# Squares for two RMS norms taken by ScalarE activations in place of GpSimd multiplications

## The chip, the cores and the metric

The kernel runs on one core of a Trainium2 chip. The core has five instruction queues that work side by side and wait for one another by semaphores: TensorE (PE, matrix products), VectorE (DVE, elementwise work), ScalarE (ACT, activations and copies), GpSimd (POOL, elementwise work here) and SyncE (SP, which issues the transfers, DMAs). Each queue runs its instructions strictly in the order in which the program lists them. The metric is the device time of one execution in microseconds (us); less is better.

## What is computed

One layer of a hybrid decoder on 1024 tokens with 1024 features, all in float32. An RMS norm and one input projection feed two groups of heads: a chunked state-space part (SSD) whose output is gated by SiLU of `z`, and an attention without softmax ("stick-breaking": sigmoids and a running product over the keys). Each group's output gets an RMS norm of its own, which needs the sum of the squares of its 1024 features for every token:

```python
y_ssd = rmsnorm(y * jax.nn.silu(z), ssd_norm_g)
y_att = stick_breaking_attention(q, k, v)
y_att = rmsnorm(y_att.reshape(b, L, D_ATT), att_norm_g)
x = x + jnp.concatenate([y_ssd, y_att], axis=-1) @ w_out
```

Then come a squared-ReLU MLP on a further norm, and a final norm. The change concerns the squares that feed `y_ssd`'s and `y_att`'s norms.

## The kernel before, in words

Activations are kept with the features on the 128 partitions and the tokens along the free axis. Every large product is made from three matrix products of split operands (a rounded part `hi` and the remainder `lo`), as in lines 161 to 163, so PE carries most of the time. Weights come from DRAM in 128x512 blocks `raw` (pool `ws`, two buffers) and are split into `whi` and `wlo`, either by POOL (lines 107 and 108) or by ACT and DVE (lines 110 and 112); a `raw` buffer is free for the next load when its remainder has been made.

**SSD stage (0 to about 380 us).** For each of four groups of heads `ssd_group` (lines 328 to 407) runs interleaved with the projections of the next group. It works through eight chunks; per chunk PE transposes, multiplies the masked decay matrix `wm` (made on DVE and ACT, line 352 is its exponential, line 353 its product with `cbm`) by the inputs, updates the running `state` (DVE, lines 389 and 392) and adds the skip term (line 402). With the last group runs `zgroup` (lines 409 to 426): the projections of the first four 128-feature blocks of `z`, one SiLU over all four (line 418), and then for each block `j` the load of that block's SSD output `yl` from DRAM (line 421, three buffers), the gating product in place in `zb` (DVE, line 422), its store (line 423), the square into `yl` (POOL, line 424) and the addition to the running sum `zacc` (POOL, line 425).

**Attention stage (about 380 to 950 us).** `qkv(hp)` projects q, k and v for a pair of heads; eight pairs follow one another. A `Group` makes the scores (lines 528 to 531), two sigmoids per tile on ACT (lines 548, 549), the running product over the keys on DVE (a scan, line 539) and a product (line 541), transposes of the weights on PE (line 599) with a split of the result on ACT and DVE (`ath`, `atl`, lines 602 and 603), and the products with v (lines 615, 616). `store` (lines 619 to 634) puts the two halves of a PSUM result together: an ACT copy into `y2` (line 628) and a DVE addition into `yt` (line 629) for each head; after the second head of the pair `yt` is stored, squared into `y2` (POOL, line 633) and added to `sacc` (POOL, line 634). There are four such places in a pair. The projections of the next pair run as filler between the attention's pieces, by a hand-made quota with costs per piece; in the eighth pair the filler is `zgate(j)` for the last four blocks of `z` (lines 636 to 650): per half of 512 tokens a load of `yl`, the projection, a sigmoid (ACT, line 644), its product with the projection (DVE, line 645), the gating product (POOL, line 646), the store, the square into `zs` (POOL, line 648) and the addition to `zacc` (POOL, line 649). `yl`, `zs` and `vt` share one set of three buffers (tag `half`), so the next half's sigmoid has to wait until an older half's last reader is done.

**After it.** `mix_operands(0)` loads and splits the first blocks of `w_out` (lines 756, 110 and 112), `mix_block(0)` multiplies them (lines 734 to 736), with the sums of four blocks left in PSUM; `token_scale(zacc)` (lines 715 to 720) turns the sums of squares into scales by way of PE, ACT and POOL, and line 783 adds each scaled PSUM block to `x1`. The norm and the MLP follow.

The framework decides the order of each engine's instructions at compile time: in the order of the text, what stands under `tc.high_priority(offset=HP)` moved 100 places forward, and by when its own model of durations has the inputs ready. The squares stand outside `high_priority`.

Of the kernel before, what the change touches and what calls it, by code (L numbers as in the profile page):

```python
# [11 lines left out]
AF = mybir.ActivationFunctionType  # L12
ALU = mybir.AluOpType
# [37 lines left out]
def trunk(ctx: ExitStack, tc, x, wct, wdt, cols, g_mix, g_mlp, g_fin, wout, wup, wdown, out):  # L51
    nc = tc.nc
    mm, act, vec, pool = nc.tensor.matmul, nc.scalar, nc.vector, nc.gpsimd
# [32 lines left out]
    def wide(name):  # L86
        return pa.tile([P, 1028], F32, name=name, tag="wide", bufs=3)
# [26 lines left out]
    def unit(src, where):  # L114

        parts = []
        for j in range(2):
            raw = ws.tile([P, 512], F32, name="raw", tag="raw", bufs=2)
            nc.sync.dma_start(out=raw, in_=src[:, j * 512:j * 512 + 512])
            hi = ws.tile([P, 512], F32R, name="whi", tag="whi", bufs=NW)  # L120
            lo = ws.tile([P, 512], F32R, name="wlo", tag="wlo", bufs=NW)
            split(raw, hi, lo, where)
            parts.append((hi, lo))
        return parts
# [26 lines left out]
    def gemm_steps(w, hhi, hlo, half, cuts=1):  # L151

        ps = bank("mm")
        m = 512 // cuts
        for q in range(cuts):
            n = slice(half * 512 + q * m, half * 512 + q * m + m)
            o = ps[:, q * m:q * m + m]
            for k in range(KT):
                whi, wlo = w[k // 4]
                wc = slice(k % 4 * P, (k % 4 + 1) * P)  # L160
                mm(out=o, lhsT=whi[:, wc], rhs=hhi[:, k, n], start=(k == 0), stop=False)  # L161
                mm(out=o, lhsT=whi[:, wc], rhs=hlo[:, k, n], start=False, stop=False)  # L162
                mm(out=o, lhsT=wlo[:, wc], rhs=hhi[:, k, n], start=False, stop=(k == KT - 1))  # L163
                if k < KT - 1 or q < cuts - 1:
                    yield
        return ps

    def gemm_half(w, hhi, hlo, half, cuts=1):
        steps = gemm_steps(w, hhi, hlo, half, cuts)
        while True:  # L170
            try:
                next(steps)
            except StopIteration as done:
                return done.value
# [234 lines left out]
    def zgroup():  # L409

        zb = pa.tile([P, 4, T], F32, name="xb", tag="xb", bufs=2)
        for j in range(NZ):
            w = unit(wct[40 + j], "pool")
            for half in range(2):
                ps = gemm_half(w, hhi, hlo, half)
                act.copy(out=zb[:, j, half * 512:half * 512 + 512], in_=ps)
                yield
        act.activation(out=zb[:, 0:NZ], in_=zb[:, 0:NZ], func=AF.Silu)
        for j in range(NZ):
            yl = wide("yl")[:, 0:T]  # L420
            nc.sync.dma_start(out=yl, in_=ysp[j])
            vec.tensor_tensor(out=zb[:, j, :], in0=zb[:, j, :], in1=yl, op=ALU.mult)
            nc.sync.dma_start(out=ygt[j], in_=zb[:, j, :])
            pool.tensor_tensor(out=yl, in0=zb[:, j, :], in1=zb[:, j, :], op=ALU.mult)
            pool.tensor_tensor(out=zacc, in0=zacc, in1=yl, op=ALU.add)
            yield

# [11 lines left out]
    for g in range(4):  # L439
        drive(ssd_group(g, *made[-1]), conv_group(g + 1) if g < 3 else zgroup(), 0.8 if g == 3 else 0.6)  # L440
# [72 lines left out]
    class Group:  # L513
# [106 lines left out]
        def store(self, r, yp):  # L620
            hp, g = self.hp, self.g
            rows = slice(r * 64, r * 64 + 64)
            if r == 0:
                yts[hp, g] = (pb.tile([P, 256], F32, name="yt", tag="yt", bufs=2),
                              pb.tile([P, 256], F32, name="y2", tag="y2", bufs=2))
            yt, y2 = yts[hp, g]
            with tc.high_priority(offset=HP):
                act.copy(out=y2[rows], in_=yp[64:128])
                vec.tensor_tensor(out=yt[rows], in0=yp[0:64], in1=y2[rows], op=ALU.add)
            if r == 1:  # L630
                n = slice(g * 256, g * 256 + 256)
                nc.sync.dma_start(out=ygt[8 + hp, :, n], in_=yt)
                pool.tensor_tensor(out=y2, in0=yt, in1=yt, op=ALU.mult)
                pool.tensor_tensor(out=sacc[:, n], in0=sacc[:, n], in1=y2, op=ALU.add)

    def zgate(j):
        w = unit(wct[40 + j], "pool")
        for half in range(2):
            n = slice(half * 512, half * 512 + 512)
            yl = pb.tile([P, 512], F32, name="yl", tag="half", bufs=NH2)  # L640
            nc.sync.dma_start(out=yl, in_=ysp[j, :, n])
            ps = yield from gemm_steps(w, hhi, hlo, half)
            zs = pb.tile([P, 512], F32, name="zs", tag="half", bufs=NH2)
            act.activation(out=zs, in_=ps, func=AF.Sigmoid)
            vec.tensor_tensor(out=zs, in0=ps, in1=zs, op=ALU.mult)
            pool.tensor_tensor(out=yl, in0=yl, in1=zs, op=ALU.mult)
            nc.sync.dma_start(out=ygt[j, :, n], in_=yl)
            pool.tensor_tensor(out=zs, in0=yl, in1=yl, op=ALU.mult)
            pool.tensor_tensor(out=zacc[:, n], in0=zacc[:, n], in1=zs, op=ALU.add)
            yield  # L650

# [31 lines left out]
    for k in range(len(slots) + LATE):  # L683
        if k < len(slots):
            n, r, b = slots[k]
            hp, at = divmod(k, nslot)
            if at == 0:
                if fill is not None:
                    for _ in fill:
                        run_later()  # L690
                fill = qkv(hp + 1) if hp < 7 else chain(*[zgate(j) for j in range(NZ, 8)])
                nfill = 48 if hp < 7 else (8 - NZ) * 16
                done, used = 0, 0.0
                length = (25.6 + nfill * 0.65) / nslot
            parts = [(0.44, lambda: groups[n].turn(r, b))] + ahead.get(k, [])
        else:
            parts, at = [], nslot - 1
        if k >= LATE:
            n0, r0, b0 = slots[k - LATE]
            parts.append((0.44, lambda: groups[n0].product(r0, b0)))  # L700
        used += sum(c for c, _ in parts)
        quota = min(nfill, max(done, ((at + 1) * length - used) / 0.65))
        had = done
        for i, (_, step) in enumerate(parts):
            step()
            while done + 0.5 < had + (quota - had) * (i + 1) / len(parts):
                next(fill, None)
                run_later()
                done += 1
# [13 lines left out]
    def accumulate(ahl, whl, store, lag=0):  # L723

        late = []
        for tt in range(8):
            for nh in range(2):
                ps = bank("a")
                n = slice(nh * 512, nh * 512 + 512)
                t = slice(tt * P, (tt + 1) * P)  # L730
                nk = len(ahl)
                for k in range(nk):
                    (ah, al), (wh, wl) = ahl[k], whl[k]
                    mm(out=ps, lhsT=ah[:, t], rhs=wh[:, n], start=(k == 0), stop=False)  # L734
                    mm(out=ps, lhsT=ah[:, t], rhs=wl[:, n], start=False, stop=False)  # L735
                    mm(out=ps, lhsT=al[:, t], rhs=wh[:, n], start=False, stop=(k == nk - 1))  # L736
                late.append((ps, tt, n))
                if len(late) == max(1, lag):
                    yield
                    store(*late.pop(0))  # L740
        for args in late:
            store(*args)
# [532 lines left out]
```

## Time and profile before

| | us |
|---|---|
| median of 3 runs (1786.0 to 1787.95) | 1786.34 |
| the profiled execution | 1790.58 |
| its span, first to last instruction | 1788.8 |
| PE busy | 1719.3 |
| DVE busy | 1288.9 |
| ACT busy | 794.7 |
| POOL busy | 572.3 |

The span is what the trace covers; the execution's own time is 1.78 us more. Busy time is the union of an engine's instructions, waiting not counted, but an instruction that is held up after its start counts as busy. An idle time is put down to the instruction whose end came last. The chain of waits goes from the last instruction back to what released it, step by step.

### The profile page before, as it was taken

Reading aid. Unit: us, or ns where it says so; the run is one execution under the profiler, and the core shown is the slowest. Engines: PE = TensorE matmul, PEld = TensorE weight load, DVE = VectorE, ACT = ScalarE, POOL = GpSimd, SP = SyncE. Lnnn points to the kernel's source line nnn. Section 1 sums busy time; section 2 is a strip of 40 time slices with the busy share of each in tenths; the row PEclk is TensorE's granted clock in tenths of the full one; section 3 lists DMA queues with packets and bytes.
Section 4 is the critical chain, followed back from the end, with each engine's and each line's share of the span. In section 5 each row is a group of like instructions: output and inputs, shape, how many; then the busy total and the mean of one; then the engine's idle time right before and its main releaser. Section 6 shows DMA issues by size and latency. Waiting matters only on the chain.

```text
span 1788.8 us, 23877 instructions
## 1 busy us (share of the span) xinstructions
PE 1719.3 (96%) x8492; PEld 1401.2 (78%) x8492; DVE 1288.9 (72%) x1771; ACT 794.7 (44%) x1516; POOL 572.3 (32%) x645
## 2 busy tenths in 40 slices
PE   6999999989999999999989999999999999999997
PEld 5778878767778778778778788778888877888886
DVE  6587886559797888888775665967666656687775
ACT  5232123316566556556542221544455446444443
POOL 6222222154454454554575331410212210010221
PEclk9999999989999999999999999999999999999999
DMA  4101102120011111110135221455433448854554
GB/s 156 36 30 53 56 28 95 59 83 30 30 33 34 35 35 33 33 32 31 58 119 206 95 100 66 151 172 205 160 141 142 151 160 303 292 159 149 165 169 147
DMA packets 90840, 189.40 MB, mean 106 GB/s; under 512 B 10080, under 2 KB 14432, under 8 KB 90720
## 3 DMA queue, kind: packets, MB, share of 16 engines
q1 hardware_dynamic: 90576, 187.61, 30.7%
q8 instruction: 67, 1.10, 0.3%
q14 instruction: 53, 0.43, 0.1%
q10 hardware_dynamic: 144, 0.26, 0.0%
HBM read 137.50 MB, written 50.33 MB: 105 GB/s over the span
## 4 chain that ended last, share of the span: by engine, by line
PE 77%; DVE 13%; POOL 3%; ACT 3%; issue 2%; DMA 2%; SPq 0%; DVEq 0%; POOLq 0%; ACTq 0%
PE ps_mm L163 7%; PE ps_mm L161 7%; PE ps_mm L162 7%; DVE m L539 5%; PE ps_a L1179 4%; PE ps_a L1181 4%; PE ps_a L1180 4%; PE ps_a L734 3%; PE ps_a L736 3%; PE ps_a L735 3%; PE ps_x L987 3%; PE ps_x L986 2%; PE ps_x L985 2%; DVE a L541 2%; PE ps_tr L599 2%
## 5 line engine op out<-in xcount | busy, mean ns | idle before, releaser
L161 PE MATMUL ps_mm<-hhi,whi 128*128 128x512 f32 (+1 forms) x784 | 322.7, 412 | 0.1
L163 PE MATMUL ps_mm<-hhi,wlo 128*128 128x512 f32 (+1 forms) x784 | 309.4, 395 | 0.0
L162 PE MATMUL ps_mm<-hlo,whi 128*128 128x512 f32 (+1 forms) x784 | 308.5, 393 | 0.0
L539 DVE TENSOR_TENSOR_SCAN m<-m 128x512 f32<-128x512 f32 (+7 forms) x128 | 181.1, 1439 | 26.6 <-ACT m L548 26.4
L163 PEld LDWEIGHTS ps_mm<-hhi,wlo 128*128 128x128 f32 x784 | 148.9, 190 | 32.2 <-issue 2.4
L161 PEld LDWEIGHTS ps_mm<-hhi,whi 128*128 128x128 f32 x784 | 149.6, 191 | 20.1 <-issue 2.9
L162 PEld LDWEIGHTS ps_mm<-hlo,whi 128*128 128x128 f32 x784 | 149.6, 191 | 18.5 <-issue 1.4
L112 POOL TENSOR_TENSOR wlo<-wf,whi 128x512 fp32r<-128x512 f32 x48 | 65.8, 1372 | 245.7 <-ACT whi L110 245.7
L107 POOL TENSOR_SCALAR whi<-raw 128x512 fp32r<-128x512 f32 x90 | 66.4, 738 | 218.9 <-PE ps_mm L162 206.2
L108 POOL TENSOR_TENSOR wlo<-raw,whi 128x512 fp32r<-128x512 f32 x90 | 133.6, 1484 | 7.4
L783 DVE SCALAR_TENSOR_TENSOR x<-ps_a,rr,x 128x512 f32<-128x512 f32 x128 | 93.7, 748 | 55.7 <-PE ps_a L736 46.5
L110 ACT CAST op<-raw 128x512 fp32r<-128x512 f32 x131 | 77.9, 620 | 117.0 <-issue 54.8
L603 DVE TENSOR_TENSOR atl<-ps_tr,ath 128x512 fp32r<-128x512 f32 (+1 forms) x160 | 100.6, 630 | 35.2 <-ACT ath L602 33.4
L112 DVE TENSOR_TENSOR op<-raw,op 128x512 fp32r<-128x512 f32 x131 | 93.0, 731 | 41.6 <-ACT op L110 41.2
L548 ACT ACTIVATE m<-ps_a 128x384 f32<-128x384 f32 (+1 forms) x192 | 95.9, 500 | 32.8 <-PE ps_a L531 29.0
L1179 PE MATMUL ps_a<-op 128*128 128x512 f32 x278 | 108.3, 390 | 1.8 <-ACT uP L951 1.8
L599 PE MATMUL ps_tr<-ident,a 128*128 128x128 f32 x576 | 91.6, 275 | 18.6 <-DVE atl L603 10.2
L1181 PE MATMUL ps_a<-op 128*128 128x512 f32 x278 | 108.2, 389 | 0.0
L1180 PE MATMUL ps_a<-op 128*128 128x512 f32 x278 | 108.2, 389 | 0.0
L602 ACT CAST ath<-ps_tr 128x512 fp32r<-128x512 f32 (+1 forms) x160 | 86.8, 544 | 44.0 <-PE ps_tr L599 40.6
L1136 POOL TENSOR_TENSOR x<-x,raw 128x512 f32<-128x512 f32 x16 | 24.5, 1537 | 253.8 <-DVE x L1144 113.7
L599 PEld LDWEIGHTS ps_tr<-ident,a 128*128 128x128 f32 x576 | 70.6, 140 | 41.6 <-DVE atl L603 14.1
(365 smaller groups left out, 4341.7 us busy)
## 6 DMA issues: line engine op xcount, KB each, us to landing
raw<-ub SPq DMA_DIRECT2D x112, 256.0 KB, 3.2
raw<-in_wct_dram SPq DMA_DIRECT2D x96, 256.0 KB, 2.6
wf<-in_wup_dram SPq DMA_DIRECT2D x38, 512.0 KB, 3.5
raw<-in_wdown_dram SPq DMA_DIRECT2D x68, 256.0 KB, 3.4
ub<-v SPq DMA_DIRECT2D x48, 256.0 KB, 2.0
raw<-in_wout_dram SPq DMA_DIRECT2D x32, 256.0 KB, 2.8
yl<-ygt SPq DMA_DIRECT2D x16, 512.0 KB, 3.9
ub<-uP SPq DMA_DIRECT2D x32, 256.0 KB, 2.0
```

Of the source, the lines that this page charges most:

```text
L108: pool.tensor_tensor(out=lo, in0=raw, in1=hi.bitcast(F32), op=ALU.subtract)
L112: e.tensor_tensor(out=lo, in0=raw, in1=hi.bitcast(F32), op=ALU.subtract)
L161: mm(out=o, lhsT=whi[:, wc], rhs=hhi[:, k, n], start=(k == 0), stop=False)
L162: mm(out=o, lhsT=whi[:, wc], rhs=hlo[:, k, n], start=False, stop=False)
L163: mm(out=o, lhsT=wlo[:, wc], rhs=hhi[:, k, n], start=False, stop=(k == KT - 1))
L539: vec.tensor_tensor_scan(mv, mv, mv, 1.0, ALU.mult, ALU.min)
L548: act.activation(out=m[:, o:o + w], in_=src, func=AF.Sigmoid, scale=-1.0)
L599: nc.tensor.transpose(out=tp[:, o:o + P], in_=a[:, c:c + P], identity=ident)
L603: vec.tensor_tensor(out=tl[:, o:], in0=tp[:, o:], in1=th[:, o:].bitcast(F32), op=ALU.subtract)
L1179: mm(out=ps, lhsT=o[0][:, t], rhs=o[2], start=first, stop=False)
L1180: mm(out=ps, lhsT=o[0][:, t], rhs=o[3], start=False, stop=False)
L1181: mm(out=ps, lhsT=o[1][:, t], rhs=o[2], start=False, stop=last)
```

## The change

Three POOL multiplications of a tile with itself become ACT activations with the function Square; sources, destinations and everything around them stay.

```diff
@@ zgroup
             vec.tensor_tensor(out=zb[:, j, :], in0=zb[:, j, :], in1=yl, op=ALU.mult)
             nc.sync.dma_start(out=ygt[j], in_=zb[:, j, :])
-            pool.tensor_tensor(out=yl, in0=zb[:, j, :], in1=zb[:, j, :], op=ALU.mult)
+            act.activation(out=yl, in_=zb[:, j, :], func=AF.Square)
             pool.tensor_tensor(out=zacc, in0=zacc, in1=yl, op=ALU.add)
@@ Group.store
                 nc.sync.dma_start(out=ygt[8 + hp, :, n], in_=yt)
-                pool.tensor_tensor(out=y2, in0=yt, in1=yt, op=ALU.mult)
+                act.activation(out=y2, in_=yt, func=AF.Square)
                 pool.tensor_tensor(out=sacc[:, n], in0=sacc[:, n], in1=y2, op=ALU.add)
@@ zgate
             nc.sync.dma_start(out=ygt[j, :, n], in_=yl)
-            pool.tensor_tensor(out=zs, in0=yl, in1=yl, op=ALU.mult)
+            act.activation(out=zs, in_=yl, func=AF.Square)
             pool.tensor_tensor(out=zacc[:, n], in0=zacc[:, n], in1=zs, op=ALU.add)
```

## Rows read from the trace of the kernel before

**Rows 1.** The page: busy time by engine; the chain that ended last, by engine.

```profile
PE 1719.3 (96%) x8492; PEld 1401.2 (78%) x8492; DVE 1288.9 (72%) x1771; ACT 794.7 (44%) x1516; POOL 572.3 (32%) x645
PE 77%; DVE 13%; POOL 3%; ACT 3%; issue 2%; DMA 2%; SPq 0%; DVEq 0%; POOLq 0%; ACTq 0%
```

**Rows 2.** Stage windows: us; PE, PEld, DVE, ACT, POOL busy (instructions); PEclk, DMA share, GB/s.

```profile
345.00:400.00 55.00, 46.83 (x213) 37.41 (x212) 34.08 (x45) 15.24 (x21) 27.04 (x17) 0.91 0.25 96
646.40:711.80 65.40, 63.42 (x369) 51.98 (x368) 55.52 (x67) 40.55 (x91) 31.84 (x45) 1.00 0.11 33
865.00:953.00 88.00, 83.12 (x447) 68.50 (x445) 58.49 (x67) 39.41 (x86) 63.15 (x60) 0.96 0.32 104
```

**Rows 3.** The same windows in steps of 5 us, the end of the SSD.

```profile
355.00:360.00 5.00, 2.59 (x15) 1.89 (x13) 5.00 (x3) 0.54 (x3) 4.92 (x3) 1.00 0.49 197
375.00:380.00 5.00, 2.05 (x6) 1.76 (x7) 3.73 (x5) 0.58 (x1) 2.44 (x2) 0.52 0.30 105
```

**Rows 4.** POOL's lines 424 and 425: duration ns min/median/max, first and last start.

```profile
L424 POOL TENSOR_TENSOR yl<-xb x4: 1892/2204/2807, 354.1 to 371.9; 128x1024 f32<-128x1024 f32 x4
L425 POOL TENSOR_TENSOR zacc<-zacc,yl x4: 2375/2667/3235, 357.0 to 373.9; 128x1024 f32<-128x1024 f32 x4
```

**Rows 5.** The chain of waits, 355 to 378 us: start, us, what.

```profile
355.15 5.06 DVE wm L353 x2
...
368.06 1.98 DVE state L389
...
372.50 4.60 DVE wlo L112 x2
```

**Rows 6.** DVE's lines 353 and 389 over the whole span: duration ns min/median/max.

```profile
L353 DVE TENSOR_TENSOR wm<-wm,cbm x32: 676/679/2826, 99.9 to 357.4; 128x512 f32<-128x512 f32 x32
L389 DVE TENSOR_TENSOR state<-state,cdn x24: 406/416/2062, 106.1 to 368.0; 128x256 f32<-128x256 f32 x24
```

**Rows 7.** ACT's squares (lines 135, 951) and last table load: ns min/median/max, first and last start.

```profile
L135 ACT ACTIVATE sq<-xq x8: 1056/1060/1078, 4.2 to 23.3; 128x1024 f32<-128x1024 f32 x8
L951 ACT ACTIVATE uP<-uP x16: 631/633/636, 1202.0 to 1456.2; 128x512 f32<-128x512 f32 x16
L548 ACT ACT_TABLE_LOAD  x1: 1283/1283/1283, 404.7 to 404.7; - x1
```

**Rows 8.** POOL 881 to 915 us, by line: busy us, mean ns; and one wait, 860:960.

```profile
L648 POOL TENSOR_TENSOR zs<-yl 128x512 f32<-128x512 f32 x3 | 6.2, 2062 | 0.2
...
ACT zs L644 <- POOL zacc L649: 12.4, 5, 3.8
```

**Rows 9.** 905 to 923 us: the chain's DMA; ACT's timeline; two windows.

```profile
912.59 3.05 DMA raw<-in_wout_dram
...
915.66 0.62 ACT L110 CAST kl<-raw 128x512 fp32r<-128x512 f32 x1 [10.59 <-DMA raw<-in_wout_dram]
...
913.00:918.00 5.00, 1.50 (x9) 0.97 (x7) 1.44 (x3) 2.29 (x5) 1.72 (x4) 1.00 0.45 157
918.00:923.00 5.00, 3.76 (x11) 2.62 (x12) 4.80 (x6) 3.29 (x8) 4.23 (x3) 0.50 0.53 165
```

**Rows 10.** POOL 925 to 953 us by line; DVE's timeline at the stage's end.

```profile
L648 POOL TENSOR_TENSOR zs<-yl 128x512 f32<-128x512 f32 x4 | 6.0, 1503 | 0.2
...
956.91 2.72 DVE L783 SCALAR_TENSOR_TENSOR x<-ps_a,rr,x 128x512 f32<-128x512 f32 x4 [8.56 <-POOL rr L129]
```

**Rows 11.** Attention, 405 to 865 us, by line: busy us, mean ns; one wait, 400:860.

```profile
L633 POOL TENSOR_TENSOR y<-yt 128x256 f32<-128x256 f32 x27 | 21.2, 783 | 37.2 <-DVE yt L629 36.6
...
L539 DVE TENSOR_TENSOR_SCAN m<-m 128x896 f32<-128x896 f32 x14 | 33.1, 2363 | 11.6 <-ACT m L548 11.6
L539 DVE TENSOR_TENSOR_SCAN m<-m 128x1024 f32<-128x1024 f32 x14 | 31.9, 2281 | 0.0
...
POOL y L633 <- DVE yt L629: 36.6, 14, 3.6
```

## The prediction

> **What bounds the kernel now.** I read the page first: PE is busy 96% of the span and holds 77% of the chain that ended last; POOL has 3% of it [rows 1]. So POOL's work is worth something only where PE stands still because of it. The view of busy time by stages shows where that is. A head pair of the attention takes 65.40 us with 369 matmuls, 28.2 in 5 us, and PE idle for only 2.0 us; the end of the SSD (345 to 400 us) has 213 matmuls in 55 us, and the eighth pair (865 to 953 us) has POOL busy for 63 of 88 us [rows 2]. Both odd stretches hold squares that the change moves.
>
> In the first, steps of 5 us show PE busy for 2.59 us while POOL is busy for 4.92 and DVE for all of it, and later for 2.05 us [rows 3]. POOL runs four squares and four additions there, 4 x 2.2 and 4 x 2.7 = 19.5 us, nearly without a pause [rows 4]. The chain names DVE in this time: two products L353 take 5.06 us, one L389 takes 1.98, two L112 take 4.60 [rows 5]. L353 has a median of 0.68 us over its 32 calls and L389 of 0.42 [rows 6]; L112 has L353's shape and kind. So DVE is not slow by its own work: instructions with two operands in SBUF stretch by the length of a POOL instruction when POOL is at work. The excess on the chain is (5.06 - 1.36) + (1.98 - 0.42) + (4.60 - 1.36) = 8.5 us.
>
> In the second stretch the trouble is one queue. ACT stood for 10.59 us before a cast of `w_out`, for a DMA issued at 912.59 [rows 9]. That DMA needs a `raw` buffer, which POOL's split of the last `z` weights frees, and POOL came to that split late, behind the gating products, squares and additions of three halves. All else in ACT's queue stood behind the cast, so PE got 9 + 11 matmuls in 10 us instead of 56, and lost 36 x 5 / 28.2 = 6.4 us; the granted clock in the second half of it was 0.50, that is 1.2 in place of 2.4 GHz, after the idle time [rows 9].
>
> **The change part by part.** The sum is made against the profiled execution, 1790.58 us, of which 1788.8 are span; it is 4.24 us (0.24%) above the median 1786.34, and I carry the difference in time over to the median unchanged.
>
> *Price of a square on ACT.* 128x1024 takes 1.06 us, 128x512 takes 0.63 [rows 7]; for 128x256 I go down the same line, 0.63 - 0.21 = 0.42. The function costs no table load beside the sigmoids: L951 squares at 1202 us and later, and the last load was at 404.7 [rows 7]. Next to SiLU and Exp, in the first stretch, the trace shows no square; the bound is none to two loads of 1.28 us, on an engine busy 15 of 55 us [rows 2], and I take none. The Trainium skill (ScalarE: Activation LUTs, "Table sets: the hidden batching unit") says that cheap functions stand in every set, but its list there (relu, copy, identity, abs) leaves out Square; read strictly it would put one or two loads of its 2.7 us here, 3 to 5 us on ACT, and the sum would be an estimated 5 to 7 in place of 10 if the path held them. No run here shows it.
>
> *End of the SSD (L424).* Four POOL squares go, 8.8 us; four ACT squares come, 4.2 us, beside work that leaves ACT idle for 40 of 55 us. If that cover is gone, 4.2 us is the loss. The wait moves: `zacc`'s addition now waits for ACT. The first square stands behind the two exponentials that L353 needs too, so the first addition starts about 1.06 us after them, and the two L353 (1.36 us) run mostly alone: their 3.7 us of excess goes. The other 4.8 us shrink with POOL's time, from 19.5 to 10.7 us, so by 45%, 2.2 us. Together 5.9 us; I take **5**, since a square may also be listed ahead of a copy that the chain needs. The ends: a gain of 8.5 us plus about 2 for the lower clock (0.52 granted from 375 to 380 us, half of 5 us [rows 3]), or a loss of 4.2.
>
> *Eighth pair (L648 and its L633).* Of POOL's work from 881 to 915 us three squares go, 6.2 us [rows 8], and two of L633, 0.78 each [rows 11]. The additions have to wait for ACT, 0.63 each: 6.2 + 1.6 - 1.9 = 5.9 us earlier at the split that frees the buffer. That is the whole lost 6.4 us if ACT's queue keeps its order. But the order is planned with shorter POOL times too, which pulls the casts of `w_out` forward in ACT's queue, and the rest of POOL's lateness (stretched products and additions) stays. I take 4, between 0 and 6.4. At the end of the stage the four last squares take 6.0 us on POOL [rows 10] and would take 2.5 on ACT; the path from the last square through `zacc` to the scale is what DVE's L783 waited for, 8.56 us by then [rows 10]. PE has other matmuls for most of this, so I take 1 of 3.5. ACT gains 8 x 0.63 = 5 us on 39 of 88. The added wait, for POOL's gating product, has the attention's casts queued behind it; but ACT already waits there for the later addition (12.4 us in five places [rows 8]), so the new wait largely takes the front part of the old one. Together **5**.
>
> *The other seven pairs (L633).* Per pair four squares: 4 x 0.78 = 3.1 of POOL's 31.8 us go, 4 x 0.42 = 1.7 us come to ACT's 40.6 of 65.4. Stretching exists here: a scan of 896 takes 2.36 us, one of 1024 only 2.28 [rows 11]; at 7/8 of the latter it would be 2.00, so 14 x 0.36 = 5 us over seven pairs. The squares' share of POOL's time is 10%, half a microsecond in all. The addition L634 now waits for ACT, with POOL's weight splits behind it; POOL is half idle and hides that. I take **0**. The ends: a gain of 7 x 2.0 = 14 us, all of PE's idle time, or a loss of 28 x 0.42 = 11.8, every square on the path. No DMA is moved on SP's queue or past any other; their waits come earlier or stay.
>
> Sum: 5 + 5 + 0 = **10 us**: 1780.6 for the profiled execution, 1776 for the median.
>
> **The rivals.**
> - *One stretch only.* If the planner pulls the casts forward by all that POOL saves, PE's stop near 915 us stays and only the SSD's 5 us are gained: 1781. For it: the cast had been planned 10 us before its data were there. Against: half of POOL's lateness was the stretched squares themselves.
> - *The attention gains too.* If the four squares of a pair each hold up a DVE instruction on the path, PE's idle 2.0 us a pair go as well: 1776 - 14 = 1762. For it: the excess of the scans. Against: only a tenth of POOL's time there is squares, and the excess found is 5 us in all. The Trainium skill (SBUF — State Buffer, "SBUF: two separate sides") has a rule for this rival: DVE and GpSimd share a port pair under an exclusive lock, and the loser is blocked for the other's whole instruction. That would put up to a square's full length on DVE each time; the trace agrees in kind (2.8 us at most for an L353 of 0.68 [rows 6]), and the scans show that most squares here meet no such instruction.
> - *Nothing.* DVE collides with the additions instead, as long as before, and the order of ACT gives back the rest: 1786.
> - *Slower: ACT waits at its head.* A square listed soon after L628 waits for DVE's addition L629, which can stand behind a scan of 2.3 us; POOL, in the square's old place, waited for it 36.6 us in 14 places, 3.6 at the longest [rows 11]. Behind it in ACT's queue stand `ath` casts and sigmoids, for which DVE and PE wait. From the point where the 28 squares cost their 0.42 us each on the path, this is 11.8 us, against 4 left in the two stretches: 1794. Against: ACT is idle 38% of a pair, and the order is planned so that the addition is done first.
>
> **How the numbers follow.** Both stretches gain, 0.48, with 1768 to 1780 by the sums above. One stretch only 0.20, attention too 0.07, nothing 0.12, slower 0.13. A measurement of this kernel tells a difference of about 0.2%, 3.6 us. Faster is 0.48 + 0.20 + 0.07 = 0.75, the same 0.12, slower 0.13. The range leaves out the two outer rivals (0.07 + 0.13) and takes in the others with the bounds of the terms: 1765 to 1789.
>
> **What would show it.** In the changed trace the two L353 near 355 us should be near 0.7 us each and L112 near 372 us below 4.6 for two; PE should have over 213 matmuls in the 55 us from 345; ACT's longest wait for `w_out` should be well below 10.6 us and the stop of PE near 915 us short; a pair should still take 65.4 us. If a pair takes longer by more than 0.5 us, the squares are on the attention's path and the prediction falls; if PE stops as long near 915 us, the one-stretch rival holds.

## The result, and the profile after

The changed kernel takes 1776.1 us (median of 6 runs, 1772.97 to 1778.29) against 1787.14 us for the kernel before in the same comparison: a ratio of 0.9932 with a 95% interval of 0.9921 to 0.9944, 11 us less. The forecast of 1776 was met; two of its three terms were not, and the errors cancelled, which is luck.

The page of the changed kernel, the rows that answer [rows 1]:

```profile
PE 1710.7 (97%) x8492; PEld 1396.8 (79%) x8492; DVE 1276.8 (72%) x1771; ACT 813.8 (46%) x1560; POOL 518.5 (29%) x601
PE 81%; DVE 10%; POOL 2%; ACT 2%; DMA 2%; issue 2%; SPq 0%; DVEq 0%; POOLq 0%; ACTq 0%
```

POOL lost 54 us of work and ACT gained 19, but what counts is that DVE's share of the chain shrank from 13% to 10% and PE's rose from 77% to 81%. Stage windows, as in [rows 2] and [rows 3]: the end of the SSD, a head pair, the eighth pair (10 us earlier now), and steps of 5 us (us; PE, PEld, DVE, ACT, POOL busy with instructions; PEclk, DMA share, GB/s):

```profile
345.00:400.00 55.00, 52.95 (x264) 42.67 (x262) 30.82 (x55) 25.13 (x38) 24.67 (x23) 1.00 0.30 106
628.45:693.90 65.45, 63.38 (x370) 51.95 (x369) 55.25 (x68) 41.75 (x95) 27.54 (x40) 1.00 0.10 33
855.00:943.00 88.00, 83.95 (x457) 68.95 (x455) 56.67 (x67) 45.59 (x99) 47.60 (x48) 0.98 0.32 108
355.00:360.00 5.00, 5.00 (x34) 4.48 (x32) 4.60 (x9) 3.59 (x6) 3.99 (x2) 1.00 0.44 175
375.00:380.00 5.00, 5.00 (x24) 4.14 (x23) 1.38 (x2) 1.19 (x2) 1.92 (x2) 1.00 0.00 0
873.00:878.00 5.00, 3.16 (x14) 2.30 (x13) 2.91 (x4) 1.48 (x3) 4.46 (x6) 0.87 0.14 52
878.00:883.00 5.00, 5.00 (x23) 4.00 (x23) 2.18 (x3) 2.40 (x6) 3.01 (x6) 0.79 0.29 105
```

In the 55 us from 345 PE now does 264 matmuls instead of 213, at full clock throughout. A pair is as it was. In the eighth pair PE's stop near 915 us is gone, but two new windows, 14 and 23 matmuls at 0.87 and 0.79 of the clock, stand near 875 us.

To find where the 11 us lie, the starts of the same instructions are compared. The first q of the attention (L493) moves from 385.8 to 375.3 us, 10.5 earlier (10.2 if measured from the last L416 before the stretch). The first sigmoid of the eighth pair (L644) moves from 877.9 to 868.3, so the attention gave back 0.9 in this profile. The first L717 moves from 952.8 to 941.9, so the eighth pair gained 1.3. From the first L783 on both programs list the same order; there the profiled execution of after was another 6.7 us shorter (825.2 us against 831.9), which makes the two profiled executions differ by more than the medians do.

**The end of the SSD.** DVE's lines there, 345 to 386 us before and 345 to 376 us after (busy us, mean ns, then idle time before them). First before:

```profile
L422 DVE TENSOR_TENSOR xb<-xb,yl 128x1024 f32<-128x1024 f32 x4 | 6.1, 1557 | 1.2 <-ACT xb L418 1.2
L112 DVE TENSOR_TENSOR wlo<-raw,whi 128x512 fp32r<-128x512 f32 x4 | 6.0, 1530 | 0.9 <-ACT whi L110 0.9
L353 DVE TENSOR_TENSOR wm<-wm,cbm 128x512 f32<-128x512 f32 x2 | 5.1, 2604 | 0.0
L389 DVE TENSOR_TENSOR state<-state,cdn 128x256 f32<-128x256 f32 x2 | 3.3, 1664 | 0.0
```

and after:

```profile
L422 DVE TENSOR_TENSOR xb<-xb,yl 128x1024 f32<-128x1024 f32 x4 | 4.8, 1215 | 1.2 <-ACT xb L418 1.2
L389 DVE TENSOR_TENSOR state<-state,cdn 128x256 f32<-128x256 f32 x2 | 2.9, 1458 | 0.0
L112 DVE TENSOR_TENSOR wlo<-raw,whi 128x512 fp32r<-128x512 f32 x4 | 2.6, 681 | 0.9 <-ACT whi L110 0.9
L353 DVE TENSOR_TENSOR wm<-wm,cbm 128x512 f32<-128x512 f32 x2 | 1.3, 682 | 0.0
```

By the means, L353 gives 2 x 1.92 = 3.8 us, L112 4 x 0.85 = 3.4, L422 4 x 0.34 = 1.4 and L389 2 x 0.21 = 0.4: 9.0 us. L389 alone is still stretched. The rest of the gain is clock. DVE's timeline from the last skip term (L402) to the first q, before and after:

```profile
378.68 0.87 DVE L402 SCALAR_TENSOR_TENSOR yt<-xb,colt,ps_tr 128x256 f32<-128x256 f32 x2 [0.78 <-PE ps_tr L397]
386.44 0.68 DVE L494 SCALAR_TENSOR_TENSOR q<-ps_mm,q 64x512 fp32r<-64x512 f32 x1 [6.89 <-ACT q L493]
```

```profile
369.87 0.87 DVE L402 SCALAR_TENSOR_TENSOR yt<-xb,colt,ps_tr 128x256 f32<-128x256 f32 x2 [0.53 <-PE ps_tr L397]
375.95 0.68 DVE L494 SCALAR_TENSOR_TENSOR q<-ps_mm,q 64x512 fp32r<-64x512 f32 x1 [5.20 <-ACT q L493]
```

L402 comes 8.8 us earlier (8.5 from the last L416), and the way from it to q, PE work alone, takes 5.20 us instead of 6.89: before, PE came to it after standing still and ran it at a granted clock of 0.52 [rows 3] and then 0.79, now at 1.00. The second step before was

```profile
380.00:385.00 5.00, 5.00 (x19) 3.97 (x19) 0.00 (x0) 0.59 (x1) 0.00 (x0) 0.79 0.53 210
```

So about 8.5 us are DVE's stretching and 1.7 the clock. The parting is not exact: the two transposes L397 just ahead of L402 took 0.69 us before and 0.44 after, which is PE's too.

**The eighth pair.** Waits, 860 to 950 us (us in total, times, longest), which answer [rows 8] and [rows 9]:

```profile
ACT zs L648 <- POOL yl L646: 13.7, 7, 2.7
ACT kl L110 <- DMA raw<-in_wout_dram: 4.9, 2, 3.6
ACT zs L644 <- POOL zacc L649: 1.0, 1, 1.0
```

The wait for `w_out` shrank from 10.6 us at the longest to 3.6, and the sigmoid's wait from 12.4 us to 1.0. In its place stands the Square's wait for POOL's gating product, 13.7 us. The chain of waits at the new stop near 875 us shows its price:

```profile
871.56 2.68 POOL yl L646
...
874.25 0.63 ACT zs L648
...
874.91 0.38 ACT y L628
...
875.31 0.43 DVE yt L629
...
875.78 0.38 PE ps_b L615
```

ACT's copy L628 waited for nothing but the Square ahead of it, which waited for POOL. Behind L628 come DVE's addition and PE's next product with v, for which PE stood 1.84 us. The lower clock in the two windows is not a fixed part of that price. A second profile of the changed kernel (after_again) has the same stop, with PE busy for the same 3.16 us, and kept the full clock behind it:

```profile
876.00:881.00 5.00, 3.16 (x19) 2.34 (x17) 2.92 (x4) 1.48 (x3) 4.46 (x6) 1.00 0.14 52
881.00:886.00 5.00, 5.00 (x32) 4.10 (x30) 3.65 (x4) 2.40 (x6) 4.59 (x6) 1.00 0.49 154
```

### The profile page after: what moved, and what is told of

It reads as the page before. It is cut to its first block, busy times and chain, and to the rows that moved or that the text cites. A ratio compares the mean times of both kernels' runs of the same rounds, so it can differ in the third digit from the quotient of the medians.

```text
span 1771.3 us, 23843 instructions
## 1 busy us (share of the span) xinstructions
PE 1710.7 (97%) x8492; PEld 1396.8 (79%) x8492; DVE 1276.8 (72%) x1771; ACT 813.8 (46%) x1560; POOL 518.5 (29%) x601
## 4 chain that ended last, share of the span: by engine, by line
PE 81%; DVE 10%; POOL 2%; ACT 2%; DMA 2%; issue 2%; SPq 0%; DVEq 0%; POOLq 0%; ACTq 0%
PE ps_mm L161 8%; PE ps_mm L163 8%; PE ps_mm L162 8%; PE ps_a L1179 4%; PE ps_a L1181 4%; PE ps_a L1180 4%; DVE m L539 4%; PE ps_a L734 3%; PE ps_a L736 3%; PE ps_a L735 3%; PE ps_tr L599 3%; PE ps_x L987 3%; PE ps_x L985 3%; PE ps_x L986 3%; DVE a L541 2%; PE ps_mm L987 2%
## 5 line engine op out<-in xcount | busy, mean ns | idle before, releaser
L108 POOL TENSOR_TENSOR wlo<-raw,whi 128x512 fp32r<-128x512 f32 x90 | 138.3, 1537 | 7.4
L112 POOL TENSOR_TENSOR wlo<-wf,whi 128x512 fp32r<-128x512 f32 x48 | 65.4, 1364 | 243.2 <-ACT whi L110 243.2
L783 DVE SCALAR_TENSOR_TENSOR x<-ps_a,rr,x 128x512 f32<-128x512 f32 x128 | 93.7, 748 | 56.0 <-PE ps_a L736 46.8
L112 DVE TENSOR_TENSOR op<-raw,op 128x512 fp32r<-128x512 f32 x131 | 91.0, 716 | 37.3 <-ACT op L110 36.9
```

The source lines that it names most:

```text
L108: pool.tensor_tensor(out=lo, in0=raw, in1=hi.bitcast(F32), op=ALU.subtract)
L112: e.tensor_tensor(out=lo, in0=raw, in1=hi.bitcast(F32), op=ALU.subtract)
```

## The experiments

All times are medians, and the ratios are to the kernel before on the same chip. q is the start of the first L493, pair the period of the scans over 1024 columns from about 565 to 830 us, and last pair the time from the first L644 to the first L717.

| kernel | us | ratio, interval | q | pair | last pair |
|---|---|---|---|---|---|
| before | 1787.14 | 1 | 385.8 | 65.40 | 74.9 |
| after | 1776.10 | 0.9932, 0.9921 to 0.9944 | 375.3 | 65.46 | 73.6 |
| after_again | 1777.38 | 0.9946, 0.9932 to 0.9960 | 375.7 | 65.45 | 72.6 |
| z_only | 1778.20 | 0.9948, 0.9930 to 0.9965 | 375.0 | 65.39 | 75.5 |
| s_only | 1788.30 | 0.9999, 0.9989 to 1.0009 | 385.6 | 65.45 | 73.5 |
| g_only | 1786.72 | 0.9987, 0.9977 to 0.9996 | 386.3 | 65.38 | 74.8 |
| z_s | 1778.71 | 0.9948, 0.9934 to 0.9962 | 374.7 | 65.45 | 73.4 |
| z_dummy_mult | 1783.60 | 0.9970, 0.9959 to 0.9982 | 381.4 | 65.39 | 75.5 |
| z_dummy_set | 1783.56 | 0.9977, 0.9968 to 0.9986 | 379.1 | 65.40 | 75.6 |
| g_vec | 1773.87 | 0.9924, 0.9910 to 0.9938 | 375.0 | 65.45 | 69.5 |
| g_vec_s | 1773.27 | 0.9921, 0.9907 to 0.9934 | 376.7 | 65.39 | 70.2 |
| g_vec_add | 1780.56 | 0.9968, 0.9955 to 0.9980 | 380.4 | 65.45 | 69.6 |
| s_three | 1783.47 | 0.9979, 0.9968 to 0.9989 | 375.2 | 66.97 | 73.1 |

**One line at a time.** z_only changes L424 alone, s_only L633 alone, g_only L648 alone:

```diff
# z_only (against before)
-            pool.tensor_tensor(out=yl, in0=zb[:, j, :], in1=zb[:, j, :], op=ALU.mult)
+            act.activation(out=yl, in_=zb[:, j, :], func=AF.Square)
# s_only (against before)
-                pool.tensor_tensor(out=y2, in0=yt, in1=yt, op=ALU.mult)
+                act.activation(out=y2, in_=yt, func=AF.Square)
# g_only (against before)
-            pool.tensor_tensor(out=zs, in0=yl, in1=yl, op=ALU.mult)
+            act.activation(out=zs, in_=yl, func=AF.Square)
```

> Only L424 goes to ACT. Theory A (the end of the SSD carries nearly all of the gain, because DVE is no longer held up by POOL): first q cast (L493) near 375.5 us instead of 385.8, a pair at 65.40 us, PE's stop near 915 us in full, total 10 us below before. Theory B (the prediction's split, half and half): L493 near 380 to 381, total 5 us below before.

> Only L633 goes to ACT. Theory A (the squares cost ACT's queue a little in the attention): a pair at 65.43 to 65.47 us, the first zgate sigmoid (L644) 0.5 to 1 us later than before (877.9), total 0 to 1 us above before. Prediction's value: pair unchanged, total 0. Rival (attention gains): a pair below 65 us.

> Only L648 goes to ACT. Theory A (a new wait at ACT's head for POOL's L646 gives back what the earlier w_out cast gains): ACT waits 10 to 14 us in all for L646, the wait for w_out falls from 10.6 to below 5 us, from the first L644 to the first zacc product on PE (L717) about 73.5 us against 74.9 before, total 1 to 2 us below before. Theory B (prediction): total 5 us below before.

By the medians L424 alone gives 10.1 us (1788.31 to 1778.2), L633 nothing, L648 1.6: 11.7 in sum, near the whole. Nearly all of the change's worth is four instructions in 20 us of the SSD's end. In z_only the stop near 915 us is there in full (ACT waits 10.5 us for `w_out`), as its theory A said. L633 lengthens a pair by 0.05 us, 0.4 us in seven. In s_only the first L644 comes 3.3 us later than before, where theory A named 0.5 to 1; its profile has a granted clock of 0.50 from 435 to 440 us, where the profile before has 1.00. In the last pair it is L633 that shortens the time, by 1.4 us (73.5 against 74.9; two profiles of the changed kernel differ by 1.0), with 7.6 us instead of 10.6 as the longest wait for `w_out`. L648 doesn't shorten it (74.8, where theory A named 73.5), although there the wait for `w_out` fell as forecast. So the rows of g_only don't show where its 1.6 us lie. In g_only:

```profile
ACT zs L648 <- POOL yl L646: 14.5, 7, 2.6
ACT kl L110 <- DMA raw<-in_wout_dram: 5.4, 2, 3.6
```

**Is it POOL's time, or what POOL reads?** z_dummy_mult keeps the gain's edit and gives POOL an unread product of the same size back; z_dummy_set gives it two fills instead, which write the same tile but read nothing.

```diff
# z_dummy_mult (against z_only)
             pool.tensor_tensor(out=zacc, in0=zacc, in1=yl, op=ALU.add)
+            pool.tensor_tensor(out=yl, in0=zb[:, j, :], in1=zb[:, j, :], op=ALU.mult)
# z_dummy_set (against z_only)
             pool.tensor_tensor(out=zacc, in0=zacc, in1=yl, op=ALU.add)
+            pool.memset(yl, 0.0)
+            pool.memset(yl, 0.0)
```

> As z_only, and after each addition L425 POOL multiplies zb by itself into yl again, which nobody reads. Theory A (it is POOL's mere presence that stretches DVE's instructions with two SBUF operands): most of the gain goes, L493 first at 383 to 387 us, L353 or L389 or L112 stretched again, total within 3 us of before. Rival (the gain came from zacc's chain being shorter, not from DVE): L493 stays near 375.5 to 376.5 us and the total 9 to 10 us below before.

> The L424 square on ACT as in the run with that line alone, and behind each addition L425 two POOL fills of the finished square's tile with zeros (about 0.95 us each, read by nobody): POOL is busy as long as with a square of its own, but with an instruction that reads nothing from SBUF. Theory A (any POOL instruction holds up DVE's two-operand products): as with the unread POOL product, about 5 of the 10 us are given back, first q (L495) at 381 to 382 us, total 1782 to 1784. Theory B (only a POOL instruction that reads two operands from SBUF does it): nothing is given back, first q at 375 to 376 us, total 1777 to 1779, L112 and L389 as in the run with that line alone.

With the unread product, q came at 381.4, so 6 of the 10 us were gone again, less than theory A named (383 to 387 us, and a total within 3 us of before, where 4.7 were left). The two L353 ran ahead of it and kept their 1.29 us; the fourth L422 and the two L112 were stretched again. Counted from the last L416, L402 comes 3.7 us later than in z_only; the rest of the 6 is the lower clock that followed (0.65 and 0.67 in the two steps from 370 us). The total for the fills is the same 1783.6, which is what theory A forecast for them, and it misleads; their q, at 379.1, is in neither theory. DVE's timeline of z_dummy_mult at 364 to 372 us:

```profile
364.86 2.10 DVE L422 TENSOR_TENSOR xb<-xb,yl 128x1024 f32<-128x1024 f32 x1
...
367.56 4.48 DVE L112 TENSOR_TENSOR wlo<-raw,whi 128x512 fp32r<-128x512 f32 x2
```

The same instructions in z_dummy_set, with an L389 before them, and POOL in the same time:

```profile
362.10 0.41 DVE L389 TENSOR_TENSOR state<-state,cdn 128x256 f32<-128x256 f32 x1
...
366.30 1.23 DVE L422 TENSOR_TENSOR xb<-xb,yl 128x1024 f32<-128x1024 f32 x1 [3.12 <-DMA yl<-ysp]
...
368.11 1.29 DVE L112 TENSOR_TENSOR wlo<-raw,whi 128x512 fp32r<-128x512 f32 x2
```

```profile
362.02 1.85 POOL L425 MEMSET yl<- 128x1024 f32 x2
363.83 2.38 POOL L425 TENSOR_TENSOR zacc<-zacc,yl 128x1024 f32<-128x1024 f32 x1
366.13 2.87 POOL L425 MEMSET yl<- 128x1024 f32 x3
```

POOL's fills run beside L389, L422 and the first L112, and none of them is stretched (0.41, 1.23, and 1.29 for two L112). With the unread product, POOL runs nothing but additions and products, and L112 takes 4.48 for two and L422 2.10. A late load is not the cause there: DVE stood only 0.06 us ahead of that L422. So what holds DVE up here is a POOL instruction that reads two operands from SBUF, not a busy POOL; one that reads a single operand was not tried. By the Trainium skill (SBUF — State Buffer, "Who interferes with whom") a DVE instruction with two SBUF inputs contends with a GpSimd instruction that reads SBUF and not with one that only writes it; these rows agree. The 4 us that the fills cost are another thing: they hold a `yl` buffer longer, the load of the fourth block is issued at 363.0 us (359.1 in z_only), and DVE's fourth gating product waits 3.12 us for it, after which PE runs at 0.50 for 5 us:

```profile
370.00:375.00 5.00, 4.51 (x12) 3.66 (x13) 1.30 (x3) 1.17 (x2) 4.40 (x4) 0.50 0.84 302
```

**What L648 is worth beside the other two.** z_s is the changed kernel with L648 back on POOL.

```diff
# z_s (against after)
-            act.activation(out=zs, in_=yl, func=AF.Square)
+            pool.tensor_tensor(out=zs, in0=yl, in1=yl, op=ALU.mult)
```

> The changed kernel with L648 alone put back on POOL, to see what that line is worth beside the two others. Theory A (its gain at the cast of w_out is eaten by ACT's new wait for the gating product): total within 2 us of the changed kernel's, L644 to L717 within 1.5 us of 73.6, ACT's longest wait for a block of w_out back at 7 to 10 us. Theory B (the prediction's term of 5 us): total 4 to 6 us above the changed kernel's.

It took 1778.71 us, the changed kernel on the same chip 1777.38, and its last pair was 73.4 us against 73.6 and 72.6, with 7.6 us as the longest wait for `w_out`: theory A. L648 is worth about 1 us here, less than these runs can tell from nothing.

**Is the Square's wait at the head of ACT's queue what took L648's gain?** g_vec removes the stretched product that it waits for: L646 goes to DVE.

```diff
# g_vec (against after)
-            pool.tensor_tensor(out=yl, in0=yl, in1=zs, op=ALU.mult)
+            vec.tensor_tensor(out=yl, in0=yl, in1=zs, op=ALU.mult)
```

> The changed kernel with zgate's gating product (L646) on DVE in place of POOL. Theory A (the stops of PE near 875 us come from ACT's Square standing at the head of its queue for POOL's stretched gating product): ACT's wait for the source of L648 falls from 13.7 us to below 8, first L644 to L717 from 73.6 us to about 71, total 2 to 4 us below the changed kernel. Theory B (DVE is the tight engine of the eighth pair, and eight more products of 0.7 us on it cost what the wait gives back): L644 to L717 stays at 73 to 75 us, total as the changed kernel's.

Theory A, with more than it asked for: 1773.87 us, 3.5 below the changed kernel on the same chip, and the last pair at 69.5 us, 3 to 4 less. Waits, 860 to 945 us:

```profile
ACT zs L648 <- DVE yl L646: 5.1, 6, 2.3
```

POOL's additions wait longer for ACT (23.8 us in all), which costs nothing; ACT waits 5.1 us instead of 13.7. ACT's timeline where it stood 2.69 us before:

```profile
871.20 0.37 ACT L628 COPY y<-ps_b 64x256 f32<-64x256 f32 x1
871.85 0.63 ACT L648 ACTIVATE zs<-yl 128x512 f32<-128x512 f32 x1 [0.28 <-DVE yl L646]
```

In this kernel L628 is listed ahead of the Square, so the edit moved the order too; it removes POOL's product and that place in the order together, and the runs don't part the two. DVE runs the eight products (6.6 us) without PE losing by it. g_vec is faster than both kernels.

**Did L633 pay once that was done?** g_vec_s puts it back on POOL.

```diff
# g_vec_s (against g_vec)
-                act.activation(out=y2, in_=yt, func=AF.Square)
+                pool.tensor_tensor(out=y2, in0=yt, in1=yt, op=ALU.mult)
```

> The kernel with the gating product L646 on DVE, and L633 alone put back on POOL. Theory A (L633 on ACT costs 0.05 us a pair and gains nothing): a pair back at 65.40 us, total within 1 us of the kernel with the gating product on DVE, so no measurable difference. Theory B (L633 on ACT pays once the eighth pair is freed, because POOL's two squares there stretch DVE's scans): first L644 to L717 is 1.5 us or more above the 69.6 us of that kernel, total 1 to 3 us above.

1773.27 us against 1773.87, the pair back at 65.39 us, the last pair 0.6 longer: theory A.

**Could POOL's last share go as well?** g_vec_add puts zgroup's additions on DVE.

```diff
# g_vec_add (against g_vec)
-            pool.tensor_tensor(out=zacc, in0=zacc, in1=yl, op=ALU.add)
+            vec.tensor_tensor(out=zacc, in0=zacc, in1=yl, op=ALU.add)
```

> The kernel with the gating product L646 on DVE, and zgroup's four additions L425 also on DVE, so that POOL does nothing of zgroup. Theory A (the additions still stretch two L389 to 1.0 and 1.9 us, and PE lacks 2.0 us between 360 and 370 us for it): both L389 at 0.41 us, PE's gap goes, first q at 373 to 374.5 us, total 1 to 2 us below. Theory B (DVE, busy for 13 of the 15 us from 355 on, pays the additions of 1.2 us itself): first q at 376 us or later, total 0 to 4 us above.

Theory B, and beyond its upper end: 6.7 us above g_vec, q at 380.4. Both L389 are at 0.41 us now, but four additions of 1.21 us stand in DVE's queue between products that PE waits for:

```profile
365.00:370.00 5.00, 2.67 (x17) 1.73 (x15) 5.00 (x10) 1.21 (x2) 0.00 (x0) 1.00 0.23 93
370.00:375.00 5.00, 3.26 (x10) 2.67 (x10) 2.57 (x6) 0.58 (x1) 0.00 (x0) 0.56 0.57 215
```

With POOL at 0.00, DVE is busy for all of the first 5 us by its own work and PE does 17 matmuls; then the clock falls to 0.56. Here the contention was removed, and the work that went to the engine that had been held up cost more than that gave.

**How near was the slower rival?** s_three issues every Square of L633 three times.

```diff
# s_three (against after)
-                act.activation(out=y2, in_=yt, func=AF.Square)
+                act.activation(out=y2, in_=yt, func=AF.Square)
+                act.activation(out=y2, in_=yt, func=AF.Square)
+                act.activation(out=y2, in_=yt, func=AF.Square)
```

> The changed kernel with each Square of L633 issued three times in a row on ACT (the same result written again), so four times two more squares of 0.42 us in every pair, ACT 45 of 65.4 us busy. Theory A (ACT has room in a pair, and a square costs the path almost nothing): a pair takes 65.4 to 65.7 us, total within 3 us of the changed kernel's. Theory B (the rival of the prediction: squares at the head of ACT's queue hold up the casts and sigmoids on the path): each added square is paid in full, 8 x 0.42 = 3.4 us a pair, a pair near 68.8 us, total about 24 us above the changed kernel's.

Between the two theories, outside the numbers of both: a pair takes 66.97 us, 1.5 more for 8 x 0.42 = 3.4 us of squares, so 45% of their length is paid; the total is 6 to 7 us above the changed kernel's. The chain of waits of one pair has them on it:

```profile
646.89 0.43 DVE yt L629
647.35 0.43 ACT y L633
647.79 0.43 ACT y L633
648.25 0.42 ACT y L633
648.69 0.58 ACT kh L500
649.29 0.49 ACT ath L602
649.90 0.52 PE ps_tr L599 x3
```

The Square stands right ahead of casts that PE waits for, as the rival said, though ACT is busy for only 44 of 67 us. One square at that place fits nearly into the slack (0.06 us a pair); three do not.

**Is the tail's 6.7 us the change's?**

> The changed kernel once more, for a second profile. Theory A (the 6.6 us by which the part after L783 was shorter in the changed kernel's profile is variation from run to run, the order there being the same): the ratio is again 0.993 to 0.994, the part from L783 to the end anywhere from 825 to 833 us, the first q again at 375 us and a pair at 65.45 us. Theory B (the change shortens that part): it is again within 1 us of 825 us.

The changed kernel again: 0.9946 (the expectation named 0.993 to 0.994), q at 375.7, a pair of 65.45, and the part after L783 took 1779.3 - 948.0 = 831.3 us against 825.2 in its other profile: theory A. That part varies from execution to execution, and so does the start of the attention: from the first scan to the first over 1024 columns took 35.1 us in one profile of the changed kernel (396.5 to 431.65) and 37.7 in the other (396.8 to 434.55). There the rows show what differs, the granted clock, first in after and then in after_again:

```profile
425.00:430.00 5.00, 5.00 (x30) 3.99 (x29) 4.80 (x5) 3.81 (x9) 1.00 (x3) 1.00 0.08 26
```

```profile
425.00:430.00 5.00, 5.00 (x17) 4.08 (x17) 2.97 (x5) 2.56 (x7) 1.13 (x3) 0.50 0.08 26
```

So the time that the attention gives back depends on the execution too: from q to the first L644 take 492.1 us before, 493.0 in after and 495.7 in after_again. What makes the part after L783 vary was not tried.

## Why the prediction was right, and where it was not

- **The number.** 10 us forecast, 11 measured. The terms 5, 5 and 0 came out as about 10, 1 to 2 and 0. The total was right because one term was too small by about what the other was too large, and that is luck: both stretches were named rightly, and neither size was. The lower ends 1768 and 1765 stand without a sum; the largest gains named for the two stretches, 10.5 and 6.4 + 3.5, would give 1766.
- **End of the SSD, "I take 5".** The mechanism holds: with L424 on ACT the stretching goes, with an unread POOL product it comes back, and with POOL fills it doesn't. The size failed in three places. "The other 4.8 us shrink with POOL's time, ... by 45%, 2.2 us" was wrong: the excess did not shrink in proportion. L112, 3.2 us of that excess, met it no more, since POOL then waited 3.56 us before its fourth addition; L389 kept most of its own. L422, stretched too (1.4 us), was missing from the sum, because the chain's rows were taken and not all of DVE's. And the clock, named at about 2 us for the end of the range, measured 1.7 and should have been in the value. The upper end, 10.5, was nearly the answer (10.2 measured from L416).
- **No table load.** ACT ran L424 next to SiLU and Exp with the same two loads as before, at 347.51 and 352.45 us, and none of its own. The strict reading of the Trainium skill (ScalarE: Activation LUTs, "Table sets: the hidden batching unit"), by which Square could need a load, does not hold here.
- **Eighth pair, "I take 4" and 1 for the tail.** The stop near 915 us went away as argued. The step that failed is "so the new wait largely takes the front part of the old one". In sum it does (13.7 + 1.0 us for 12.4), but the old wait stood ahead of a sigmoid, and the new one stands also ahead of L628 and the casts behind it, for which PE waits: the two windows near 875 us lack (28.2 - 14) + (28.2 - 23) = 19 matmuls, 3.4 us. With the full clock of after_again they lack (28.2 - 19) + (28.2 - 32) = 5, 1.0 us, so the clock that fell in one of the two profiles is 2.4 of the 3.4 by the matmuls, and 1.7 by its grants of 0.87 and 0.79. g_vec, which takes the POOL product out of ACT's way and changes ACT's order with it, gets 3 to 4 us back. The path at the stage's end shows no gain of its own: from L717 to L783 it is 4.1 us before and after.
- **Other pairs, "I take 0".** Right: 0.06 us a pair. The reason given, that ACT is idle 38% of a pair, was weaker than it looked: of the eight more squares in s_three, 1.5 of 3.4 us were paid, so a place in the queue has room for about two squares on average, not three.
- **Rivals.** "One stretch only" was the nearest in kind, with the stretches' parts changed: it is the SSD that gained, by twice the 5 us, and the eighth pair that hardly did, for another reason than the planner's. "The attention gains too" and "slower" are refuted by the pair's 65.46 us, "nothing" by the end of the SSD.

## What to carry to other kernels

Where one engine's instructions are far above their own median, sum all of its excess in that stretch (not only what the chain lists) and ask of each instruction whether it will still meet the other engine; the proportional cut gave 2.2 us here, where L112 alone gave 3.2. When work moves to an in-order queue, what counts is not how idle that engine is but what it now waits for at its head and who stands behind it there; moving the producer that it waits for, as g_vec does, was worth 3.5 us here, more than the move of L648 itself (about 1). Judge a control by its rows, not by its total: the fills gave the total of theory A without its mechanism, by a load that came late.

## What was not expected of the hardware

The clock can fall in one of two kernels with the same idle time ahead of it. In g_vec and g_vec_s DVE's instructions at the end of the SSD have the same lengths, and PE is busy for 4.36 and 3.59 us, against 4.33 and 3.59, of the two 5 us steps from 360. Yet the next step, first in g_vec and then in g_vec_s, is

```profile
370.00:375.00 5.00, 5.00 (x23) 4.13 (x22) 0.41 (x2) 0.59 (x2) 1.09 (x2) 1.00 0.59 232
```

```profile
370.00:375.00 5.00, 5.00 (x17) 3.91 (x17) 0.56 (x2) 0.59 (x1) 1.24 (x2) 0.68 0.64 251
```

a mean granted clock of 1.00 against 0.68 (part of the step at 1.2 in place of 2.4 GHz), 23 matmuls against 17, and the first q 1.7 us later. PE's longer idle times just ahead are alike too: 0.64, 0.43 and 0.98 us from 364 us on in g_vec, and 0.67, 0.43 and 0.98 in g_vec_s. So the same idle time was followed by the full clock once and by the lower one once, and what decided it stays open. One and the same program shows it as well: after and after_again differ so at the stop near 875 us and at the start of the attention, where PE is busy for 2.19 us of the 5 from 420 us in both. The 1.7 us by which q differs between g_vec and g_vec_s are as much as the clock's part in this change.
